# Attention in a two-layer trunk: the token norm moves from the values to the transposed weights, copies move from VectorE to ScalarE, and two query blocks share a bank and a mask

## The chip, the cores and the metric

The kernel runs on one core of a Trainium2 chip. The metric is the device time of one execution in microseconds (us). The names of the engines are those of the profile: PE is TensorE (PEld its weight loads), DVE is VectorE, ACT is ScalarE, POOL is GpSimd, SP is the queue that issues the transfers. A difference of under 0.2% of the time (2.8 us) counts here as no change.

## The reference

The model is a trunk of two layers over 512 tokens with 16 learned meta tokens ahead of them (528 columns), model width 1024. Layer 0 mixes tokens with retention and a convolution, layer 1 with the attention that this case is about, and each mixer is followed by a squared-ReLU MLP. The attention has 16 heads of width 64. Its core, cut to what matters:

```python
hn = rmsnorm(h, norm_mix_g[layer])            # one factor per token
qkv = hn @ w_qkv; q, k, v = split(qkv, 3)
q, k = rmsnorm(q, qn_g), rmsnorm(k, kn_g)     # per head
z = einsum('bhqd,bhkd->bhqk', q, k) * d ** -0.5
valid = (key < query) & (key >= n_pad)        # strictly earlier keys
log_keep = where(valid, log_sigmoid(-z), 0)
after = cumsum(log_keep, reverse) - log_keep  # keys between this one and the query
w = where(valid, exp(log_sigmoid(z) + after), 0)
out = (w @ v) @ w_o
```

So the weight of a key is the sigmoid of its score times the product of (1 - sigmoid) over the keys that lie between it and the query. The token factor of the first rmsnorm drops out of q and k, which are normed again, and stays in v.

## The kernel before, in words

The sequence is stored in reverse, channels on partitions, so that the product over the keys between becomes a running product from left to right. The 16 meta keys are the last 16 columns. There are NQ = 4 query blocks q of P = 128 queries. Block q sees the n = 528 - 128q columns from its own diagonal on: 528, 400, 272 and 144.

Products of f32 precision are made of three float32r matmuls: each operand is split into a rounded high part (`whi`, `x2h`) and the rest (`wlo`, `x2l`). In the attention DVE rounds the weights (L286) and POOL makes the low part (L289). `gemm_parts` runs one output block of 128 channels as 8 steps of k. After each step it calls `between.step`, which advances every open chain of attention work by one piece. All engines are under a manual schedule here: each works in the order in which the program records its instructions.

The attention takes the heads in pairs p = 0 to 7. `queries(p)`, `keys(p)` and `values(p)` are three gemms that start the chains; `attend(p)` runs about one pair later, between the steps of the next pair's gemms, so that PE alternates between gemm steps and pieces of attention. Which piece falls on which step is set by the table `ATT`, built from `ZS`, `TS`, `VS`, `ES` and `MS`. For head a of the pair:

- **Z(a, q)** computes the scores of one query block in a PSUM bank (`pz`): two matmuls (high and low part of Q), and one bf16 matmul of the identity `idb` with the causal mask `caus`. A block narrower than 256 columns is widened to 256. ACT turns the bank into keep (`kp`, L1266) and sigmoid (`sp`, L1267). DVE scans `kp` into the running product `E` (L1270), multiplies (`sp`, L1272), and writes the 16 meta columns twice into `Wm` (L1275).
- **T, turn(a, kb)** transposes the weights of one key block into a bank `pw` (L1283). ACT writes the high part `wTh` (L1284), DVE the low part `wTl` (L1286), which also frees the bank.
- **V** multiplies values and weights into `po` (L1293).
- **M** transposes the meta weights of both heads into `pmt` (L1299). ACT and DVE split them into `mT` (L1300, L1304). **E** adds the meta keys' part (L1307) and writes `oT`.

The pool `pat` has four banks (tag "at"), used in turn by `pq`, `pk`, `pz`, `pw`, `pv`, `pm`, `pmt` and `pe`: a fifth use waits until all readers of the first are done. The pool `pqk` has three banks for the gemms.

`token_norm` (once, in p = 0) computes the token factor `n2rb` for all 528 columns on all partitions; `values` multiplies it into `vT` as DVE reads the gemm's bank (L1204). `done(k)` runs after each k step of the last pair's values gemm: it rounds the finished head outputs `oT` of the pairs 0 to 5 into `oSh` on DVE (L1338), and POOL makes the low part `oSl` (L1339), for the output projection that follows.

## Time and profile before

| | |
|---|---|
| median of 3 runs | 1379.52 us (1379.13 to 1380.4) |
| the profiled execution's own time | 1379.57 us |
| its span | 1377.8 us |
| attention with its output projection, about | 739 to 1034 us of the span |
| one pair of heads in the steady stretch (start of mT at 794.72, 823.76, 852.80, 881.84, 910.86, 939.91) | 29.04 us |
| granted TensorE clock, mean | 0.998 |

The terms of a prediction are made against the profiled execution; 1.8 us of its time lie around the span, and it stands 0.05 us above the median. Matmuls are pipelined, so the time from the start of one to the start of the next tells what it costs, not its duration.

### The profile page before, as it was taken

The numbers are of one execution on the slowest core, as the hardware profiler recorded it, in microseconds if no ns is written. First come the engines' busy times: TensorE is split into PE (matmuls) and PEld (weight loads), VectorE is DVE, ScalarE is ACT, GpSimd is POOL, SyncE is SP. The second block draws the span as 40 slices with busy tenths as digits, with TensorE's granted clock in tenths as the row PEclk, the third lists the DMA queues.
The fourth block names the chain that finished last, engine by engine and source line by source line (L and its number), as shares of the span: only waits on it lengthen the run. The fifth ranks groups of instructions, "written<-read, shape, count | busy, mean of one in ns | idle before, by whom it ended". The sixth has DMA issues, their size and how long they took to land.

```text
span 1377.8 us, 24561 instructions
## 1 busy us (share of the span) xinstructions
PE 1356.1 (98%) x9693; PEld 1267.4 (92%) x9693; DVE 1067.4 (77%) x1909; ACT 677.8 (49%) x1328; POOL 354.6 (26%) x414
## 2 busy tenths in 40 slices
...
DMA packets 39650, 134.08 MB, mean 97 GB/s; under 512 B 4976, under 2 KB 5104, under 8 KB 39536
## 3 DMA queue, kind: packets, MB, share of 16 engines
...
q14 instruction: 38, 0.31, 0.1%
...
## 4 chain that ended last, share of the span: by engine, by line
PE 87%; DVE 8%; ACT 2%; issue 1%; DMA 0%; POOL 0%; SPq 0%; ACTq 0%; DVEq 0%; POOLq 0%
PE mm L377 50%; PE qk L377 11%; PE pz L1261 2%; PE po L1293 1%; DVE wlo L289 1%; PE pw L1283 1%; ACT whi L286 1%; PE po L796 1%; DVE x3l L415 1%; DVE mT L1304 1%; PE po L800 1%; DVE E L1270 1%; PE po L798 1%; PE pp030S L1005 0%; PE pp020S L1005 0%
## 5 line engine op out<-in xcount | busy, mean ns | idle before, releaser
L289 POOL TENSOR_TENSOR wlo<-raw,whi 128x256 fp32r<-128x256 f32 (+1 forms) x334 | 277.1, 849 | 286.6 <-ACT whi L286 133.1
L286 ACT CAST whi<-raw 128x256 fp32r<-128x256 f32 (+1 forms) x290 | 161.3, 593 | 206.1 <-PE mm L377 124.4
L592 DVE SCALAR_TENSOR_TENSOR acc<-cx,ptm,acc 128x526 f32<-128x526 f32 (+28 forms) x232 | 157.7, 742 | 3.5 <-ACT cx L587 3.5
L377 PE MATMUL mm<-xnh,whi 128*128 128x264 f32 x640 | 135.1, 293 | 0.0
L377 PE MATMUL mm<-xnl,whi 128*128 128x264 f32 x640 | 130.2, 284 | 0.4 <-DVE xnl L706 0.3
L377 PE MATMUL mm<-xnh,wlo 128*128 128x264 f32 x640 | 129.2, 283 | 0.5 <-DVE wlo L289 0.5
L289 DVE TENSOR_TENSOR wlo<-raw,whi 128x1024 fp32r<-128x1024 f32 (+1 forms) x86 | 106.5, 1239 | 18.9 <-ACT whi L286 18.0
L377 PEld LDWEIGHTS mm<-xnh,whi 128*128 128x128 f32 x640 | 100.1, 189 | 3.3 <-issue 1.3
L377 PEld LDWEIGHTS mm<-xnl,whi 128*128 128x128 f32 x640 | 99.3, 189 | 1.6 <-DVE xnl L706 1.0
L377 PEld LDWEIGHTS mm<-xnh,wlo 128*128 128x128 f32 x640 | 98.7, 188 | 0.9 <-DVE wlo L289 0.7
L241 DVE TENSOR_TENSOR wlo<-S,whi 128x512 fp32r<-128x512 f32 x96 | 65.1, 688 | 31.2 <-ACT whi L240 29.6
L240 ACT CAST whi<-S 128x512 fp32r<-128x512 f32 x96 | 57.9, 615 | 55.4 <-DVE S L225 25.5
L429 POOL TENSOR_TENSOR n2s<-n2q,n2q 128x528 f32<-128x528 f32 x1 | 1.8, 1818 | 321.5 <-DVE wlo L289 321.5
L377 PE MATMUL qk<-x2h,whi 128*128 128x264 f32 (+1 forms) x320 | 82.8, 323 | 0.5 <-ACT kraw L1153 0.5
L1030 DVE TENSOR_TENSOR h<-mm,h 128x528 f32<-128x528 f32 (+1 forms) x48 | 33.5, 699 | 62.6 <-PE mm L377 62.5
L377 PE MATMUL qk<-x2h,wlo 128*128 128x264 f32 (+1 forms) x320 | 77.0, 306 | 0.0
L377 PE MATMUL qk<-x2l,whi 128*128 128x264 f32 (+1 forms) x320 | 76.9, 305 | 0.0
L240 ACT CAST whi<-pr 128x512 fp32r<-128x512 f32 x72 | 43.3, 618 | 46.6 <-issue 10.5
L1270 DVE TENSOR_TENSOR_SCAN E<-kp,oz 128x527 f32<-128x527 f32 (+1 forms) x64 | 61.4, 979 | 1.9 <-ACT kp L1266 1.9
L377 PEld LDWEIGHTS qk<-x2h,whi 128*128 128x128 f32 x320 | 53.4, 191 | 2.6 <-ACT kraw L1153 0.9
L377 PEld LDWEIGHTS qk<-x2h,wlo 128*128 128x128 f32 x320 | 51.5, 188 | 2.7
L377 PEld LDWEIGHTS qk<-x2l,whi 128*128 128x128 f32 x320 | 51.8, 188 | 1.1
...
## 6 DMA issues: line engine op xcount, KB each, us to landing
...
```

The costliest lines, as they stand in the source:

```text
L240: nc.scalar.copy(hi[:, ks], src)
L241: nc.vector.tensor_tensor(lo[:, ks], src, hi[:, ks].bitcast(F32), ALU.subtract)
L286: copy(hi[:, ks], raw[:, ks])
L289: eng.tensor_tensor(lo[:, ks], raw[:, ks], hi[:, ks].bitcast(F32), ALU.subtract)
L377: nc.tensor.matmul(p, a[:, k, :], b[:, sl], start=(first and t == 0), stop=(last and t == 2))
L415: nc.vector.scalar_tensor_tensor(dst[1][:, :n], src, g, dst[0][:, :n].bitcast(F32), ALU.mult, ALU.subtract)
L592: nc.vector.scalar_tensor_tensor(a, cxf[:, s:T], tap(j, s), a, ALU.mult, ALU.add)
L796: nc.tensor.matmul(po[:n, :256], st[:n, :n], vk[:n], start=True, stop=Pst is None)
L798: nc.tensor.matmul(po[:n, :256], qr[:, cs], Pst, start=False, stop=True)
L1030: nc.vector.tensor_tensor(v2(h[m][:, :n], n), ps, v2(h[m][:, :n], n), ALU.add)
L1261: nc.tensor.matmul(pz[:, :w], Q2[a][:, t, q * P:(q + 1) * P], K2[a][:, k0:k0 + w], start=(t == 0), stop=(t == 1 and i > 0))
L1270: nc.vector.tensor_tensor_scan(E[:, 1:n], kp[:, :n - 1], zero.to_broadcast([P, n - 1]), 1.0, ALU.mult, ALU.add)
```

## The change

- `token_norm` no longer computes the factor for 528 columns. It computes it for five columns `rbt` with tokens on partitions: four token blocks, and one column in which the 16 meta tokens stand four times (the copy `mac` and one more matmul feed it).
- The factor is applied to the transposed weights: `wTh`, `wTl` and `mT` are scaled by a column of `rbt` as they leave PSUM. ACT's copies become activations with a scale, DVE's subtractions become scalar_tensor_tensor. `vT` becomes a plain copy, on ACT.
- The low part of `mT` is one DVE instruction over 64 partitions in place of two over 32: the columns of `Wm` are arranged so that the low parts of both heads are neighbours. The meta values `vm` are written over all 128 partitions with a 0/1 column (`CC_HM`) as scale in place of 64x64 corners.
- The `E` and `sp` tiles of the blocks 0 and 1 become one tile, and those of 2 and 3 another, so that one DVE instruction writes the meta columns of two blocks into `Wm`.
- Blocks 3 and 2 become one piece Z(a, (3, 2)): both score matrices lie side by side in one bank (144 + 272 columns, the first no longer widened to 256) under one mask matmul of 2x128 columns. The piece runs at step 2 of the table; before, block 2 ran at step 1 and block 3 at step 3.
- `done` rounds `oSh` on ACT in place of DVE.

Three places in the order of instructions, before and after. The first is in the last pair (p = 7), where `done` runs. ACT before, from the copy of the last pair's `po` on; `qy`, `qt`, `ky` and `k7t` are the keys' and queries' norms:

```order
L1310 COPY otmp_12196<-po_12151 64x512
L452 ACT_TABLE_LOAD
L452 ACTIVATE qy_12217<-qxv_11995 128x8
L453 ACTIVATE qt_12218<-qy_12217 128x8
L452 ACTIVATE ky_12221<-kxv_11997 128x528
L453 ACTIVATE k7t<-ky_12221 128x528
L1284 CAST wTh_9188<-pw_12264 128x512
L1284 CAST wTh_9187<-pw_12270 128x384
L1284 CAST wTh_9186<-pw_12275 128x256
L1266 ACT_TABLE_LOAD
```

ACT with the change:

```order
L1379 CAST oSh_12098<-oT_9194 128x512
L1343 COPY otmp_12113<-po_12068 64x512
L1379 CAST oSh_12115<-oT_9195 128x512
L454 ACT_TABLE_LOAD
L454 ACTIVATE qy_12134<-qxv_11919 128x8
L455 ACTIVATE qt_12135<-qy_12134 128x8
L454 ACTIVATE ky_12138<-kxv_11921 128x528
L455 ACTIVATE k7t<-ky_12138 128x528
L1379 CAST oSh_12144<-oT_9196 128x512
L1379 CAST oSh_12154<-oT_9197 128x512
L1379 CAST oSh_12171<-oT_9198 128x512
L1316 ACTIVATE wTh_9186<-pw_12181,rbt 128x512
```

Five of the six `oSh` copies now stand on ACT ahead of the first `wTh`; the sixth follows the third `wTh`. DVE at the same place, before:

```order
L1338 CAST oSh_12227<-oT_9198 128x512
L1338 CAST oSh_12237<-oT_9199 128x512
L456 SCALAR_TENSOR_TENSOR qt_12218<-qt_12218,qxv_11995 128x8
L457 SCALAR_TENSOR_TENSOR qy_12217<-qt_12218,qy_12217 128x8
L1177 TENSOR_SCALAR qs_12249<-qy_12217 128x8
L1178 TENSOR_SCALAR qs_12249<-qy_12217 128x8
L286 CAST whi_12165<-raw_12167 128x256
L1338 CAST oSh_12254<-oT_9200 128x512
L1180 SCALAR_TENSOR_TENSOR k7t<-k7t,kxv_11997 128x528
L1338 CAST oSh_12280<-oT_9201 128x512
L1286 TENSOR_TENSOR wTl_9192<-pw_12264,wTh_9188 128x512
```

DVE with the change:

```order
L458 SCALAR_TENSOR_TENSOR qt_12135<-qt_12135,qxv_11919 128x8
L459 SCALAR_TENSOR_TENSOR qy_12134<-qt_12135,qy_12134 128x8
L1186 TENSOR_SCALAR qs_12166<-qy_12134 128x8
L1187 TENSOR_SCALAR qs_12166<-qy_12134 128x8
L288 CAST whi_12084<-raw_12086 128x256
L1189 SCALAR_TENSOR_TENSOR k7t<-k7t,kxv_11921 128x528
L1318 SCALAR_TENSOR_TENSOR wTl_9190<-pw_12181,rbt,wTh_9186 128x512
```

The six copies are gone from ahead of `wTl` (the first two stood further up), and `wTl` reads a column of `rbt`. The second place is a pair in the steady stretch on DVE, from the keys' last scaling on, before:

```order
L1184 SCALAR_TENSOR_TENSOR ky_10956<-kraw_10739,pt,ky_10956 128x528
L1204 TENSOR_TENSOR vT<-qk_0_10912,n2rb 128x264
L1204 TENSOR_TENSOR vT<-qk_1_10913,n2rb 128x264
L1270 SCALAR_TENSOR_TENSOR E_9178<-kp_11021,oz 128x527
L1188 TENSOR_TENSOR khl_11035<-ky_10956,khl_11035 128x528
L286 CAST whi_11042<-raw_11044 128x256
L1286 TENSOR_TENSOR wTl_9189<-pw_11050,wTh_9185 128x128
L1270 SCALAR_TENSOR_TENSOR E_9179<-kp_11053,oz 128x399
L1270 SCALAR_TENSOR_TENSOR E_9180<-kp_11061,oz 128x271
L1272 TENSOR_TENSOR sp_11022<-sp_11022,E_9178 128x512
L1275 TENSOR_TENSOR Wm_9183<-sp_11022,E_9178 128x2x16
L1272 TENSOR_TENSOR sp_11054<-sp_11054,E_9179 128x384
```

With the change:

```order
L1193 SCALAR_TENSOR_TENSOR ky_10912<-kraw_10702,pt,ky_10912 128x528
L1297 SCALAR_TENSOR_TENSOR E_9178<-kp_10978,oz 128x527
L1197 TENSOR_TENSOR khl_10991<-ky_10912,khl_10991 128x528
L288 CAST whi_10998<-raw_11000 128x256
L1318 SCALAR_TENSOR_TENSOR wTl_9187<-pw_11006,rbt,wTh_9183 128x128
L1297 SCALAR_TENSOR_TENSOR E_9178<-kp_11009,oz 128x399
L1301 TENSOR_TENSOR sp_10977<-sp_10977,E_9178 128x512
L1297 SCALAR_TENSOR_TENSOR E_9179<-kp_11030,oz 128x143
L1297 SCALAR_TENSOR_TENSOR E_9179<-kp_11031,oz 128x271
L1301 TENSOR_TENSOR sp_10977<-sp_10977,E_9178 128x384
L1307 TENSOR_TENSOR Wm_9181<-sp_10977,E_9178 128x4x16
```

The two `vT` rows are gone, one `Wm` row of 4x16 stands for two of 2x16, and the scans of 143 and 271 columns come together, behind the product of block 0. The third place is PE at the scores of block 3 in a steady pair, before (block 2, with 272 columns and a mask of its own, stood two steps earlier):

```order
L377 MATMUL qk_0_10745<-x2h_8647,wlo_10490 128x264
L377 MATMUL qk_1_10746<-x2h_8647,wlo_10490 128x264
L1261 MATMUL pz_10876<-K_30_10652,Q_30_10404 128x256 x2
L1264 LDWEIGHTS idb
L1264 MATMUL pz_10876<-caus,idb 128x128
L377 MATMUL qk_0_10745<-x2h_8649,whi_10489 128x264
L377 MATMUL qk_1_10746<-x2h_8649,whi_10489 128x264
```

With the change:

```order
L379 MATMUL qk_0_10708<-x2h_8645,wlo_10461 128x264
L379 MATMUL qk_1_10709<-x2h_8645,wlo_10461 128x264
L1265 MATMUL pz_10820<-K_30_10612,Q_30_10379 128x144 x2
L1265 MATMUL pz_10820<-K_30_10612,Q_30_10379 128x272 x2
L1280 LDWEIGHTS idb
L1280 MATMUL pz_10820<-caus,idb 128x2x128
L379 MATMUL qk_0_10708<-x2h_8647,whi_10460 128x264
L379 MATMUL qk_1_10709<-x2h_8647,whi_10460 128x264
```

Block 2 has joined block 3, and one mask matmul of 2x128 columns closes both.

The diff. Left out are the lines that Z loses (they are printed above), the memsets of `mac` (in) and `vm` (out), and the column `CC_HM` of the constants, which is 1 where partition i has (i div 32) mod 2 = a, else 0:

```diff
...
-ZS, TS, VS = (0, 1, 1, 3), (10, 10, 10, 13), (16, 18)
+ZQ, ZS, TS, VS = ((0,), (1,), (3, 2)), (0, 1, 2), (10, 10, 10, 13), (16, 18)
 ATT = {}
 for a_ in range(2):
     for q_ in range(4):
-        ATT.setdefault(12 * a_ + ZS[q_], []).append(("Z", a_, q_))
+        if q_ < len(ZS):
+            ATT.setdefault(12 * a_ + ZS[q_], []).append(("Z", a_, ZQ[q_]))
         ATT.setdefault(12 * a_ + TS[q_], []).append(("T", a_, 3 - q_))
     for i_, kb_ in enumerate(((3, 2), (1, 0))):
         ATT.setdefault(12 * a_ + VS[i_], []).append(("V", a_, kb_))
...
-    Eb = [ap1.tile([P, T - P * q], F32, name=f"E{q}") for q in range(NQ)]
+    NB = [T - P * q for q in range(NQ)]
+    E2 = [ap1.tile([P, NB[q] + NB[q + 1]], F32, name=f"E{q}") for q in (0, 2)]
+    side = lambda t, q: t[:, :NB[q]] if q % 2 == 0 else t[:, NB[q - 1]:]
+    tails = lambda t, q: t[:, P:].rearrange("p (q c) -> p q c", q=2)[:, :, NB[q] - NMETA:]
+    Eb = [side(E2[q // 2], q) for q in range(NQ)]
...
     e2t = ap1.tile([P, NQ, 2], F32, name="e2t")
+    rbt = ap1.tile([P, NQ + 1], F32, name="rbt")
+    mac = ap1.tile([P, P], F32, name="mac")
...
     def values(p):
         for sl, ps in gemm_parts("w_qkv", setE, T, each=done if p == 7 else None):
-            nc.vector.tensor_tensor(vT[:, sl], ps, rb[:, sl], ALU.mult)
+            nc.scalar.copy(vT[:, sl], ps)
...
             pm = bank(f"pm{p}")
             nc.tensor.transpose(pm[:, 0:P], vT[:, SEQ:], ident)
             m = vm[p % 2]
+            mine = lambda a: ca[:, CC_HM + a:CC_HM + a + 1]
             for a in range(2):
-                r = slice(64 * a, 64 * a + 64)
-                src = pm[r, a * 64:(a + 1) * 64]
-                nc.scalar.copy(m[r, a, 0, :], src)
+                nc.scalar.activation(m[:, a, 0, :], pm[:, a * 64:(a + 1) * 64], AF.Copy, scale=mine(a))
             yield
             for a in range(2):
-                r = slice(64 * a, 64 * a + 64)
-                src = pm[r, a * 64:(a + 1) * 64]
-                nc.vector.tensor_tensor(m[r, a, 1, :], src, m[r, a, 0, :].bitcast(F32), ALU.subtract)
+                nc.vector.scalar_tensor_tensor(
+                    m[:, a, 1, :], pm[:, a * 64:(a + 1) * 64], mine(a), m[:, a, 0, :].bitcast(F32), ALU.mult, ALU.subtract)
...
-        def Z(a, q):
-
...
+        def Z(a, qs):
+            q0 = qs[0] - qs[0] % 2
+            if qs[0] != 1:
+                Ws[a, "side", q0] = ap2.tile([P, NB[q0] + NB[q0 + 1]], F32, tag=f"sp{q0}", name=f"sp{p}{a}{q0}")
+            weights_ = Ws[a, "side", q0]
+            out = []
+            for q in qs:
+                kp = ap2.tile([P, NB[q]], F32, tag=f"kp{q}", name=f"kp{p}{a}{q}", bufs=1)
+                out.append((q, NB[q], kp, side(weights_, q)))
+            def scores(pz, q, k0, w):
+                for t in range(2):
+                    nc.tensor.matmul(pz, Q2[a][:, t, q * P:(q + 1) * P], K2[a][:, k0:k0 + w],
+                                     start=(t == 0 and q == qs[0]), stop=(t == 1 and k0 >= HT and qs == (0,)))
+            def sigmoids(pz, q, kp, sg):
+                nc.scalar.activation(kp, pz, AF.Sigmoid, scale=ys[:, 0, q, a:a + 1])
+                nc.scalar.activation(sg, pz, AF.Sigmoid, scale=ys[:, 1, q, a:a + 1])
+            if len(qs) == 2:
+                pz, off = bank(f"pz{p}{a}{qs[0]}"), 0
+                for q, n, kp, sg in out:
+                    scores(pz[:, off:off + n], q, T - n, n)
+                    off += n
+                n0 = out[0][1]
+                both = pz[:, :2 * n0].rearrange("p (b c) -> p b c", b=2)[:, :, :P]
+                nc.tensor.matmul(both, idb, caus.unsqueeze(1).to_broadcast([P, 2, P]), start=False, stop=True)
+                off = 0
+                for q, n, kp, sg in out:
+                    sigmoids(pz[:, off:off + n], q, kp, sg)
+                    off += n
             else:
...
+                (q, n, kp, sg), = out
+                for i, (k0, w) in enumerate([(0, HT), (HT, HT)] if q == 0 else [(T - n, n)]):
+                    pz = bank(f"pz{p}{a}{q}{i}")[:, :w]
+                    scores(pz, q, k0, w)
+                    if i == 0:
+                        nc.tensor.matmul(pz[:, :P], idb, caus, start=False, stop=True)
+                    off = k0 if q == 0 else 0
+                    sigmoids(pz, q, kp[:, off:off + w], sg[:, off:off + w])
+            yield
+            for q, n, kp, sg in out:
+                E = Eb[q]
+                nc.vector.tensor_tensor_scan(E[:, 1:n], kp[:, :n - 1], zero.to_broadcast([P, n - 1]), 1.0, ALU.mult, ALU.add)
+            yield
+            for q, n, kp, sg in out:
+                nx, E = n - NMETA, Eb[q]
+                nc.vector.tensor_tensor(sg[:, :nx], sg[:, :nx], E[:, :nx], ALU.mult)
+                Ws[a, q] = sg
+            if qs[0]:
+                q = q0 + 1
+                twice = wm[:, q0:q0 + 2, :, a * MW:a * MW + NMETA]
+                ends = [tails(t, q).unsqueeze(2).to_broadcast([P, 2, 2, NMETA]) for t in (weights_, E2[q // 2])]
+                nc.vector.tensor_tensor(twice, *ends, ALU.mult)
         def turn(a, kb):
...
             px = bank(f"pw{p}{a}{kb}")
             for q in range(kb + 1):
                 nc.tensor.transpose(px[:, q * P:(q + 1) * P], Ws[a, q][:, (kb - q) * P:(kb - q + 1) * P], ident)
-            nc.scalar.copy(wTh[kb][:, :nq], px[:, :nq])
-            yield
-            nc.vector.tensor_tensor(wTl[kb][:, :nq], px[:, :nq], wTh[kb][:, :nq].bitcast(F32), ALU.subtract)
+            norm = rbt[:, kb:kb + 1]
+            nc.scalar.activation(wTh[kb][:, :nq], px[:, :nq], AF.Copy, scale=norm)
+            yield
+            nc.vector.scalar_tensor_tensor(
+                wTl[kb][:, :nq], px[:, :nq], norm, wTh[kb][:, :nq].bitcast(F32), ALU.mult, ALU.subtract)
         def V(a, kbs):
             if a not in po:
...
             pm = bank(f"pmt{p}")
             for q in range(NQ):
                 nc.tensor.transpose(pm[:, q * P:(q + 1) * P], wm[:, q], ident)
-            nc.scalar.copy(mT, pm)
-            yield
-            for a in range(2):
-                lo = slice(64 * a + MW, 64 * a + 2 * MW)
-                nc.vector.tensor_tensor(mT[lo], pm[lo], mT[lo].bitcast(F32), ALU.subtract)
+            norm = rbt[:, NQ:NQ + 1]
+            nc.scalar.activation(mT, pm, AF.Copy, scale=norm)
+            yield
+            lo = slice(2 * MW, 4 * MW)
+            nc.vector.scalar_tensor_tensor(mT[lo], pm[lo], norm[lo], mT[lo].bitcast(F32), ALU.mult, ALU.subtract)
         def meta(a):
             nc.tensor.matmul(po[a], vm[p % 2][:, a], mT, start=False, stop=True)
...
     def token_norm():
-        nonlocal rb, e2
-        rb, e2 = rstd(s, "n2", True, banks=(pat, "at"))
+        nonlocal e2
+        e2 = sp.tile([P, XV], F32, tag="xv", name="n2xv", bufs=1)[:, :T]
+        s.total(e2, EPS / D, EPS * EPS, (pat, "at"))
         pe = bank("pe2")
+        nc.vector.tensor_copy(mac.rearrange("p (g m) -> p g m", g=4)[:, :, :NMETA],
+                              s.acc[:, SEQ:T].unsqueeze(1).to_broadcast([P, 4, NMETA]))
         for q in range(NQ):
             nc.tensor.matmul(pe[:, q:q + 1], s.acc[:, q * P:(q + 1) * P], ones[:, 0:1], start=True, stop=True)
+        nc.tensor.matmul(pe[:, NQ:NQ + 1], mac, ones[:, 0:1], start=True, stop=True)
         for a in range(2):
             nc.vector.tensor_scalar(e2t[:, :, a], pe[:, :NQ], EPS / D, EPS * EPS, ALU.mult, ALU.add)
+        xt = ap1.tile([P, NQ + 1], F32, name="n2xt")
+        nc.vector.tensor_scalar(xt, pe[:, :NQ + 1], 1.0 / D, EPS, ALU.mult, ALU.add)
+        rsqrt(rbt, xt, [P, NQ + 1], "n2", tag="rbt")
...
         setO.append((act.tile([P, T], F32R, tag=f"Bh{k}", name=f"oSh{k}"), act.tile([P, T], F32R, tag=f"Bl{k}", name=f"oSl{k}")))
         if k < KA:
             hi, lo = (t[:, :SEQ] for t in setO[k])
-            nc.vector.tensor_copy(hi, oT[k])
+            nc.scalar.copy(hi, oT[k])
             nc.gpsimd.tensor_tensor(lo, oT[k], hi.bitcast(F32), ALU.subtract)
-    rb = e2 = None
+    e2 = None

```

More of the change, by code (lines that the diff above doesn't have):

```diff
@@ L80 @@
 CC_CAUS = CC_BLK + P
-CC_COS = CC_CAUS + P
+CC_HM = CC_CAUS + P
+CC_COS = CC_HM + 2
 CC_SIN = CC_COS + T
@@ L1087, in clear @@
         nc.gpsimd.memset(vT[:, T:], 0.0)
-        for t in (wTh[0][:, P:], wTl[0][:, P:], vm[0], vm[1]):
+        nc.gpsimd.memset(mac, 0.0)
+        for t in (wTh[0][:, P:], wTl[0][:, P:]):
             nc.gpsimd.memset(t.bitcast(F32), 0.0)
```

33 lines of the change are left out of this document (4 added, 29 removed).

## The prediction

> **What bounds the kernel now.** I read the page's first part, then the busy times of one pair's stretch, then who waited for whom on PE, and last the time order of the engines around the longest wait. The page's first part:
>
> ```profile
> PE 1356.1 (98%) x9693; PEld 1267.4 (92%) x9693; DVE 1067.4 (77%) x1909; ACT 677.8 (49%) x1328; POOL 354.6 (26%) x414
> ```
>
> Over the span PE bounds, and DVE at 77% looks unimportant. In the attention it is not. One pair of heads, busy us of PE, PEld, DVE, ACT, POOL out of 29:
>
> ```profile
> 853.50:882.50 29.00, 28.71 (x205) 25.96 (x204) 28.59 (x67) 22.18 (x51) 10.99 (x13) 1.00 0.42 111
> ```
>
> PE and DVE are both full, ACT is at 76%. Two full engines in step show waits where one hands to the other. First PE's own idle time between 740 and 1040 us, then the waits of its weight loads between 770 and 960 (total, times, longest):
>
> ```profile
> PE pz L1261 <- DVE wTl L1286: 6.2, 1, 6.2
> PE pq L1129 <- DVE mT L1304: 1.4, 6, 0.2
> ```
> ```profile
> PEld pk L1166 <- DVE ksl L1159: 2.7, 7, 1.3
> PEld pq L1129 <- ACT wTh L1284: 2.7, 6, 0.5
> PEld pmt L1299 <- DVE Wm L1275: 1.6, 6, 0.3
> ```
>
> There is one long wait of 6.2 us, and three small ones in each pair. Without the first pair's 1.3 at `pk` these are (2.7 - 1.3 + 2.7 + 1.6) / 6 = 0.95 us per pair. I put all three down to DVE: before `pq` the page names `mT` for PE itself, and `mT` holds the bank that `pq` needs.
>
> **The long wait.** PE, then DVE, then ACT in time order (start, duration, instruction, idle before):
>
> ```profile
> 957.83 0.23 PE L1264 MATMUL pz<-caus,idb 128*128 128x128 bf16 x1
> 964.31 0.81 PE L1261 MATMUL pz<-K,Q 128*128 128x264 f32 x2 [6.25 <-DVE wTl L1286]
> ```
> ```profile
> 956.64 1.29 DVE L1338 CAST oSh<-oT 128x512 fp32r<-128x512 f32 x2
> 957.86 1.22 DVE L456 SCALAR_TENSOR_TENSOR qt<-qt,qxv 128x8 f32<-128x8 f32 x1
> ...
> 962.18 1.48 DVE L1338 CAST oSh<-oT 128x512 fp32r<-128x512 f32 x1
> 963.58 0.68 DVE L1286 TENSOR_TENSOR wTl<-pw,wTh 128x512 fp32r<-128x512 f32 x1
> ```
> ```profile
> 952.24 1.28 ACT L452 ACT_TABLE_LOAD   x1
> ...
> 955.73 0.64 ACT L452 ACTIVATE ky<-kxv 128x528 f32<-128x528 f32 x1 [1.75 <-DVE kxv L1167]
> 956.41 0.65 ACT L453 ACTIVATE k7t<-ky 128x528 f32<-128x528 f32 x1
> 956.96 1.22 ACT L1284 CAST wTh<-pw 128x512 fp32r<-128x512 f32 x3
> ```
>
> The second half of block 0's scores is the fourth bank after the 512-column `pw`, so it waits until `wTl` has read that bank. `wTh` was there by 957.6; DVE came six us later, because the `oSh` copies of `done` stand in its queue. What stretches `qt`, 8 columns in 1.22 us, I read as POOL's `oSl` at work on the same memory; POOL keeps that work.
>
> With the change the copies stand on ACT, and ACT becomes what `wTl` waits for. One `oSh` falls into idle time ahead of the table load, the second moves that load by 0.6 to 952.85. It ends at 954.1, `qy` and `qt` at 954.6. `kxv` on DVE is no longer behind two copies, so `ky` and `k7t` follow until about 955.9. Three copies at 0.59 lead to 957.7, a scaled `wTh` to 958.4, `wTl` to 959.1. PE stood still from 958.06: 1.0 us would be left of 6.25. Some stretched DVE instructions remain, so I take 1.5: **a gain of 4.7**. Bounds: 0, if DVE is as late without the copies; 6.25, if nothing is left. Next behind it stand a `pw` and block 1's scores; their banks come free with `wTl` of 384 and 256 columns, within 1.0 us of the first, and PE has a gemm step of 0.7 and the scores in between, so I cost nothing there.
>
> The wait also cost clock. Windows (length, PE busy, PEld, DVE, ACT, POOL, then the granted clock):
>
> ```profile
> 960.00:962.00 2.00, 0.00 (x0) 0.00 (x0) 1.97 (x6) 0.35 (x1) 1.42 (x3) 1.00 0.00 0
> 966.00:968.00 2.00, 2.00 (x9) 1.34 (x7) 2.00 (x4) 1.34 (x6) 1.15 (x1) 0.50 0.03 8
> 968.00:970.00 2.00, 2.00 (x8) 1.64 (x8) 2.00 (x5) 1.67 (x4) 0.67 (x1) 0.71 0.78 235
> ```
>
> From 964.31 to about 968.84 (0.71 over the last window) PE worked at half clock: 4.5 / 2 = 2.3 us. At 962, four us after its last matmul, PE still had the full clock, so a wait of 1.5 us loses none: **a gain of 2.3**, or 0 if the wait stays. The Trainium skill ("TensorE: Matmul & The Clock Gate", Part 1) states that the gate halves the clock after an idle window of about 3.4 us and returns it after a busy one; the trace agrees, and by that rule any rest under 3.4 us gives the same sum.
>
> **The pairs.** Instructions of one pair on DVE, and three on ACT (count | total, mean ns | idle):
>
> ```profile
> L1275 DVE TENSOR_TENSOR Wm<-sp,E 128x32 f32<-128x32 f32 x8 | 1.4, 180 | 0.0
> L1304 DVE TENSOR_TENSOR mT<-pmt,mT 32x512 fp32r<-32x512 f32 x2 | 1.4, 690 | 0.0
> L1286 DVE TENSOR_TENSOR wTl<-pw,wTh 128x512 fp32r<-128x512 f32 x2 | 1.4, 688 | 0.0
> L1204 DVE TENSOR_TENSOR vT<-qk,n2rb 128x264 f32<-128x264 f32 x2 | 0.8, 423 | 0.0
> L1126 DVE SCALAR_TENSOR_TENSOR qhl<-qraw,pt,qhl 128x512 fp32r<-128x512 f32 x1 | 0.7, 743 | 0.0
> ```
> ```profile
> L1124 ACT ACTIVATE qhl<-qraw,pt 128x512 fp32r<-128x512 f32 x2 | 1.4, 723 | 0.1
> L1284 ACT CAST wTh<-pw 128x512 fp32r<-128x512 f32 x2 | 1.2, 586 | 0.1
> L1153 ACT COPY kraw<-qk 128x264 f32<-128x264 f32 x2 | 0.7, 382 | 0.0
> ```
>
> DVE instructions overlap by some 0.08 us, so each costs its mean less 0.08. Off DVE: two `vT`, 2 x 0.34 = 0.68; one of two `mT`, 0.69 with no overlap at its end; four of eight `Wm`, 4 x 0.10, less 0.03 on each that stays, 0.28. Onto DVE: a subtraction with a scale column. The nearest row is `qhl`, 743 against 688, so 0.055 on each of eight `wTl`, one `mT` and two `vm`: 0.6. Bounds of this: 0, and the stretched case below. DVE sheds 1.65 - 0.6 = 1.05 and would need 28.0 us per pair. The moved scans and `ksl` change places within the same sum.
>
> PE needs the measured 29.04 less its waits of 0.95, less the masks. At block 3, time order:
>
> ```profile
> 903.18 0.40 PE L1261 MATMUL pz<-K,Q 128*128 128x256 f32 x2
> 903.42 0.23 PE L1264 MATMUL pz<-caus,idb 128*128 128x128 bf16 x1
> 903.46 0.48 PE L377 MATMUL qk<-x2h,whi 128*128 128x512 f32 x1
> 903.77 0.39 PE L377 MATMUL qk<-x2l,whi 128*128 128x512 f32 x1
> 904.00 0.39 PE L377 MATMUL qk<-x2h,wlo 128*128 128x512 f32 x1
> ```
>
> A mask costs 0.04 to the next start and delays the step behind it by 0.08 (0.31 in place of 0.23). One of four per head goes, another becomes 128 columns longer (0.06 by 512 columns in 0.23): 0.06 saved per head, up to 0.14 if the longer one hides the delay; I take 0.08, 0.16 per pair. The block-3 scores go from 256 to 144 columns. The trace has no float32r matmul that narrow. From below, transposes of 128 columns, nine in 1.14 with the last one's 0.27, start every 0.11 us; from above, an f32 product of 128 columns in the retention takes two records:
>
> ```profile
> 839.02 1.14 PE L1283 MATMUL pw<-ca,sp 128*128 128x128 f32 x9
> 135.86 0.38 PE L780 MATMUL pv<-q0r,k0r 128*128 128x128 f32 x2
> ```
>
> The second of the two starts 0.11 after the first (0.38 less its own 0.27), so the product costs 0.22 at 128 columns, 0.25 at 144. Against 0.12 now (903.18 to 903.42, two matmuls) that is 0.01 less to 0.13 more each. I take no change, since all that is known of float32r here runs at the rate of single records. The Trainium skill (the same page, Part 2, LDWEIGHTS) has a load of 128 columns take 128 / 1.2 = 107 ns whatever follows. By it the narrower matmul waits for its weights, and the narrowing is worth 0.013 x 32 = 0.4 us, a sum of 1367.4; no run here shows it.
>
> The shared bank is the fourth after that of block 0's first half, which ACT has read two steps before, so it brings no new wait.
>
> So PE needs 29.04 - 0.95 - 0.16 = 27.9 and DVE 28.0. Both could gain 1.0; engines so close still wait for each other at times, and I take 0.85 in each of six pairs: **a gain of 5.1** (bounds 0.16 x 6 = 1.0 and 1.05 x 7 = 7.4).
>
> On ACT a pair gains two `vT` copies (0.38 each by `kraw`, the same shape from the same banks) and 0.14 (723 less 586) on eleven scaled copies: 2.3, which makes 24.5 of 28. I cost this at nothing, since ACT keeps 3.5 us of waiting for PE; were that cover gone, it would be up to 2.3 per pair. `vT` on ACT stands behind `khl`, as its meta copies do now; behind it wait `wTh` and the next `kp`.
>
> **The norm.** Once, at 745 us:
>
> ```profile
> 746.23 0.95 PE L1327 MATMUL pe<-ca,n2s 128*128 128x1 f32 x8
> 755.34 0.71 DVE L1159 TENSOR_TENSOR ksl<-ksq,ksh 128x528 fp32r<-128x528 f32 x1 [2.29 <-ACT ksq L1158]
> ```
>
> One more product of one column is two of eight records in 0.8 us, 0.2, and waits some 0.1 for the copy `mac`, with the keys' gemm behind it: **a loss of 0.3**. DVE's three long instructions that go here gain nothing, since DVE idles 2.29 us before its next late product anyway.
>
> **Sum.** 1379.57 - 4.7 - 2.3 - 5.1 + 0.3 = 1367.8 for the profiled execution; the median stands 0.05 below it.
>
> **Rivals.**
> (a) The narrow scores run as two-record products: 32 x 0.13 = 4.2 more, 1372.0. For it: the f32 rows do so at 128 columns. Against: one record per matmul in every float32r row.
> (b) ACT takes over DVE's lateness: the copies ahead of `wTh` hold `wTl` as long as DVE did, so wait and half clock stay, 7.0 back, 1374.8. For it: five copies ahead of it in one queue. Against: the 1.75 us that ACT idled there.
> (c) Slower: POOL stretches the scaled subtractions, which read two operands beside PSUM, as it stretched `qt`. The price is 1.22 - 0.16 at most; at half of it, 0.5, eleven per pair cost 5.5 against 1.65 shed, +3.9 x 6 = 23, less the 7.0: 1396. It decides from 0.15 each (1.65 / 11). Against it, 232 such instructions in the convolution, PSUM and a column in, with POOL busy:
>
> ```profile
> L592 DVE SCALAR_TENSOR_TENSOR acc<-cx,ptm,acc 128x526 f32<-128x526 f32 (+28 forms) x232 | 157.7, 742 | 3.5 <-ACT cx L587 3.5
> ```
>
> (d) The change gives PE nothing in the pairs because ACT's extra 2.3 us arrive late on the same hand-overs, and (b) besides: of all gains the masks' 1.0 is left, 1379.57 + 0.3 - 1.0 = 1378.9, no change. For it: ACT would be at 88%. Against: at `pq` the page names `mT` on DVE for PE itself.
>
> **How the numbers follow.** The forecast gets 0.72, (a) 0.09, (b) 0.09, (c) 0.05, (d) 0.05. The first three cases are faster by over 0.2% (2.8 us, about what a measurement can tell from no change): 0.90; same 0.05; slower 0.05. The lower end takes 1.05 in seven pairs, the whole 6.25, the 2.3 and the first pair's 1.3: 1379.6 - 17.2 + 0.3 = 1362.7, so 1362. The upper end holds (a) and (b): 1375.
>
> **What would show it.** In the changed profile the row of PE's `pz` waiting for `wTl` should be under 2.5 us with the clock at 1.00 throughout 957 to 980; `pq` waiting for `mT` should be gone; the distance of two `mT` should be 28.0 to 28.4 us; DVE's busy share of a pair should be about 97%. Two 144-column scores should start 0.10 to 0.13 apart; 0.25 would be (a). A long wait of PE for `wTl` with ACT's `wTh` just ahead of it would be (b), a mean of `wTl` over 0.85 us at 512 columns (c). The prediction is wrong if the pairs still take 29 us.

## The result

The changed kernel takes 1370.74 us (median, 1370.28 to 1371.12) against 1379.96 for the kernel before in the same comparison: a ratio of 0.9932, interval 0.9918 to 0.9946, or 9.2 us less. Forecast were 1367.8, 11.8 less. The profiled execution took 1370.59, its span is 1368.8.

The page's first part after the change, and one pair's stretch (length, PE, PEld, DVE, ACT, POOL busy, granted clock, DMA):

```profile
PE 1351.1 (99%) x9679; PEld 1261.0 (92%) x9679; DVE 1052.7 (77%) x1848; ACT 691.4 (51%) x1350; POOL 364.4 (27%) x413
```
```profile
853.50:882.50 29.00, 29.00 (x211) 26.84 (x210) 28.14 (x64) 24.51 (x54) 11.92 (x12) 1.00 0.41 123
```

The waits of PE's own between 740 and 1040 us. The long wait for `wTl` is halved, `pq`'s wait for `mT` is gone, and `pmt` has a new one:

```profile
PE pz L1265 <- DVE wTl L1318: 3.2, 1, 3.2
PE pmt L1332 <- DVE Wm L1307: 1.4, 2, 1.1
```

Of the three small waits that PE's weight loads had in each pair (770 to 960 us) only the first pair's `pk` is left:

```profile
PEld pk L1175 <- DVE ksl L1168: 1.1, 1, 1.1
```

Where the time came from is read off one instruction that each pair has once: ACT's `mT`, here for the pairs 0, 5, 6 and 7, before and after:

```profile
793.61 0.59 ACT L1300 CAST mT<-pmt 128x512 fp32r<-128x512 f32 x1 [1.56 <-PE pmt L1299]
938.80 0.59 ACT L1300 CAST mT<-pmt 128x512 fp32r<-128x512 f32 x1 [1.63 <-PE pmt L1299]
976.24 0.59 ACT L1300 CAST mT<-pmt 128x512 fp32r<-128x512 f32 x1 [1.39 <-PE pmt L1299]
1002.24 0.59 ACT L1300 CAST mT<-pmt 128x512 fp32r<-128x512 f32 x1 [4.59 <-PE pmt L1299]
```
```profile
793.90 0.69 ACT L1334 ACTIVATE mT<-pmt,rbt 128x512 fp32r<-128x512 f32 x1 [1.31 <-PE pmt L1332]
933.75 0.69 ACT L1334 ACTIVATE mT<-pmt,rbt 128x512 fp32r<-128x512 f32 x1 [1.32 <-PE pmt L1332]
966.93 0.69 ACT L1334 ACTIVATE mT<-pmt,rbt 128x512 fp32r<-128x512 f32 x1 [2.61 <-PE pmt L1332]
992.91 0.69 ACT L1334 ACTIVATE mT<-pmt,rbt 128x512 fp32r<-128x512 f32 x1 [4.52 <-PE pmt L1332]
```

Up to pair 0 the changed kernel is 0.3 us late. A pair is (938.80 - 793.61) / 5 = 29.04 before and (933.75 - 793.90) / 5 = 27.97 after, 1.07 less. From pair 5 to pair 6 it is 37.44 before, 8.40 more than a pair, and 33.18 after, 5.21 more. This is the stretch of pair 7's values gemm with `done` and the first output blocks (the expectations below call it the last pair's). From pair 6 to pair 7 it is 26.00 and 25.98. So the gain is 6 x 1.07 = 6.4 in the pairs and 8.40 - 5.21 = 3.2 in that stretch, less 0.3 ahead of them: 9.3 up to pair 7. The spans differ by 9.0, since what follows is 0.3 longer (375.56 before, 375.89 after); why was not looked into.

The same distances for every kernel of this study, read in the same way (us). The times come from five comparisons, in which the kernel before took 1379.76 to 1380.03:

| kernel | time, median | a pair | 5 to 6 | 6 to 7 |
|---|---|---|---|---|
| before | 1379.96 | 29.04 | 37.44 | 26.00 |
| changed | 1370.74 | 27.97 | 33.18 | 25.98 |
| b_osh | 1377.58 | 29.03 | 34.24 | 26.93 |
| u_osh | 1374.43 | 27.93 | 37.02 | 25.84 |
| no_osl | 1367.63 | 27.94 | 29.85 | 26.02 |
| tiny_pool | 1371.47 | 27.94 | 33.50 | 25.92 |
| late_small | 1375.25 | 28.44 | 33.05 | 27.36 |
| u_vt | 1371.21 | 27.98 | 33.10 | 25.98 |
| no_mt | 1371.53 | 28.02 | 33.21 | 25.85 |
| u_vt_mt | 1376.31 | 28.72 | 33.89 | 26.80 |
| u_bank | 1371.55 | 28.01 | 33.15 | 26.13 |
| u_clear | 1370.15 | 27.95 | 33.13 | 26.14 |
| best | 1370.76 | 27.97 | 31.94 | 27.44 |
| best2 | 1369.36 | 27.96 | 31.89 | 26.04 |

**The long wait after the change.** PE, then DVE, POOL and ACT in time order:

```profile
952.06 0.23 PE L1291 MATMUL pz<-caus,idb 128*128 128x128 bf16 x1
955.47 0.51 PE L1265 MATMUL pz<-K,Q 128*128 128x264 f32 x2 [3.18 <-DVE wTl L1318]
...
965.67 0.41 PE L1332 MATMUL pmt<-ca,Wm 128*128 128x128 f32 x2 [1.07 <-DVE Wm L1307]
```
```profile
949.50 1.27 DVE L458 SCALAR_TENSOR_TENSOR qt<-qt,qxv 128x8 f32<-128x8 f32 x1
950.80 0.66 DVE L459 SCALAR_TENSOR_TENSOR qy<-qt,qy 128x8 f32<-128x8 f32 x1
951.49 1.21 DVE L1186 TENSOR_SCALAR qs<-qy 128x8 f32<-128x8 f32 x1
952.62 1.32 DVE L1187 TENSOR_SCALAR qs<-qy 128x8 f32<-128x8 f32 x1
...
954.67 1.66 DVE L1318 SCALAR_TENSOR_TENSOR wTl<-pw,rbt,wTh 128x512 fp32r<-128x512 f32 x3
```
```profile
948.13 2.61 POOL L1380 TENSOR_TENSOR oSl<-oT,oSh 128x512 fp32r<-128x512 f32 x2
...
951.40 2.51 POOL L1380 TENSOR_TENSOR oSl<-oT,oSh 128x512 fp32r<-128x512 f32 x2
```
```profile
950.16 1.65 ACT L1379 CAST oSh<-oT 128x512 fp32r<-128x512 f32 x3
951.71 1.51 ACT L1316 ACTIVATE wTh<-pw,rbt 128x512 fp32r<-128x512 f32 x3
```

ACT brought the first `wTh` (0.69 in the pairs) at 952.4, 0.1 after PE's last matmul was done; the prediction had 0.3. DVE came to `wTl` only at 954.67. The copies are gone from its queue, but four instructions of eight columns hold it 4.5 us. They end when POOL's instructions end: `qt` at 950.77 and the second `oSl` of its row at 950.74, the last `qs` at 953.94 and that of the next row at 953.91.

**The start.** The last sum `n2s` on POOL, before and after, and PE's wait for it:

```profile
743.84 1.34 POOL L429 TENSOR_TENSOR n2s<-n2s,n2q 128x528 f32<-128x528 f32 x1
```
```profile
744.32 1.33 POOL L431 TENSOR_TENSOR n2s<-n2s,n2q 128x528 f32<-128x528 f32 x1
```
```profile
745.71 1.16 PE L444 MATMUL n2ps<-n2s,ca 128*128 128x264 f32 x4 [0.45 <-POOL n2s L431]
```

The change had moved a fourth `wlo` ahead of this sum on POOL, which the prediction did not look at.

### The profile page after: what moved, and what is told of

Read it like the earlier page. It is cut to its first block, busy times and chain, and to the rows that moved or that the text cites. A ratio compares the mean times of both kernels' runs of the same rounds, so it can differ in the third digit from the quotient of the medians.

```text
span 1368.8 us, 24471 instructions
## 1 busy us (share of the span) xinstructions
PE 1351.1 (99%) x9679; PEld 1261.0 (92%) x9679; DVE 1052.7 (77%) x1848; ACT 691.4 (51%) x1350; POOL 364.4 (27%) x413
## 3 DMA queue, kind: packets, MB, share of 16 engines
q8 instruction: 76, 1.25, 0.4%
## 5 line engine op out<-in xcount | busy, mean ns | idle before, releaser
L291 POOL TENSOR_TENSOR wlo<-raw,whi 128x256 fp32r<-128x256 f32 (+1 forms) x334 | 287.6, 881 | 268.2 <-ACT whi L288 133.6
```

What stands on the lines that cost most here:

```text
L291: eng.tensor_tensor(lo[:, ks], raw[:, ks], hi[:, ks].bitcast(F32), ALU.subtract)
```

## The experiments

### The copies and the long wait

u_osh undoes one part of the change, b_osh does this part alone:

```diff
-            nc.scalar.copy(hi, oT[k])         # u_osh, in the changed kernel
+            nc.vector.tensor_copy(hi, oT[k])
-            nc.vector.tensor_copy(hi, oT[k])  # b_osh, in the kernel before
+            nc.scalar.copy(hi, oT[k])
```

> The changed kernel with one part undone: the copies oSh of done stand on DVE again. If the copies' place is what shortened the long wait (theory), PE's wait of pz for wTl goes from 3.2 back to about 6 us, the granted clock falls to a half behind it, and the time is 1370.7 + 3 + 2.3 = 1376 us (1374 to 1377.5). If the wait was shortened by something else in the change, such as less other work on DVE (rival), the wait stays under 4 us at full clock and the time is under 1372.

> The kernel before with one part of the change alone: the copies oSh on ACT. Theory: the long wait falls from 6.25 to 3 to 3.5 and the half clock behind it goes: 1379.9 - 3 - 2.3 = 1374.6 us (1373.5 to 1376), the pairs still 29.0 us apart. Rival: the wait needs the rest of the change too (less DVE work ahead of it), stays over 5 us with the half clock, and the time is 1378 or more.

Measured: u_osh 1374.43 (ratio 0.9962, 0.9948 to 0.9977), b_osh 1377.58 (0.9984, 0.9975 to 0.9994). The wait in u_osh, the wait in b_osh, and a window of b_osh behind it (the clock stands third from the end):

```profile
958.57 0.81 PE L1265 MATMUL pz<-K,Q 128*128 128x264 f32 x2 [6.71 <-DVE wTl L1318]
```
```profile
961.43 0.81 PE L1261 MATMUL pz<-K,Q 128*128 128x264 f32 x2 [2.93 <-DVE wTl L1286]
```
```profile
961.00:963.00 2.00, 1.57 (x5) 1.38 (x6) 2.00 (x4) 1.37 (x4) 2.00 (x3) 0.52 0.00 0
```

The theory holds in its cause: the place of the copies makes the long wait. It fails in its sizes. In the changed kernel the copies are worth 3.7 us and not 5.3 (1374.43 lies low in the range expected), since u_osh has no wait at `pmt`: what PE waits less at `pz`, it waits in part there. Alone they are worth 2.2 and not 5.3: the wait fell by 3.3 as expected, but the half clock came all the same, after a wait of 2.9 us, and 0.9 went in the following distance, where PE waits 0.7 at `po` for `mT`. The stretch from pair 5 to pair 6 is 5.21 over a pair in b_osh (34.24 - 29.03) as in the changed kernel: what the change gains in this stretch, the copies gain alone.

no_osl leaves `oSl` out, tiny_pool takes the four small instructions from DVE in the last pair:

```diff
-            nc.gpsimd.tensor_tensor(lo, oT[k], hi.bitcast(F32), ALU.subtract)   # no_osl
+            setO[k] = (setO[k][0], setO[k][0])
-            rsqrt_newton(qy, qt, qxv)            # tiny_pool, for p == 7:
+            small = nc.gpsimd                    # Newton as 2 tensor_scalar, 2 tensor_tensor,
+            small.tensor_scalar(qt, qt, -0.5, None, ALU.mult)
...
+            small.tensor_scalar(ys[:, 0], qy, -0.125, None, ALU.mult)
```

> The changed kernel without the subtractions oSl that done gives to POOL; the products that read oSl read oSh a second time, so PE's work is the same and the low halves of those six pairs are not in the output. If POOL's subtractions hold DVE's small instructions (theory), qt, qy and the two qs fall from 0.66 to 1.32 us each to about 0.2, the wait of pz for wTl falls from 3.2 to 0.5 to 1.0, the 1.4 us of pmt waiting for Wm behind it to under 0.5, and the time is 1366 to 1368.5. If what is left of the wait is ACT's copies ahead of wTh (rival), the wait stays over 2.5 and the time is 1370 or more.

> The changed kernel with the last pair's four small instructions (the Newton step of qy and the two qs) as six on POOL in place of DVE; POOL keeps oSl. Theory (DVE's lateness at the long wait is those four, 4.5 us held by POOL): the wait of pz for wTl falls from 3.2 to 0.5 to 1.5, pmt's wait for Wm to under 0.7, and the time is 1367 to 1369. Rival: the next DVE instructions (whi, k7t) are held in their place, the wait falls by 1 us at most, and the time is 1369.8 or more.

Measured: no_osl 1367.63 (0.9914, 0.9900 to 0.9929), tiny_pool 1371.47 (0.9943, 0.9928 to 0.9957). Two small instructions and the wait in no_osl; then, in tiny_pool, PE's longest total wait and POOL's `qy`:

```profile
948.92 0.38 DVE L458 SCALAR_TENSOR_TENSOR qt<-qt,qxv 128x8 f32<-128x8 f32 x1 [0.46 <-ACT qt L455]
...
949.53 0.17 DVE L1186 TENSOR_SCALAR qs<-qy 128x8 f32<-128x8 f32 x1
```
```profile
953.07 0.51 PE L1265 MATMUL pz<-K,Q 128*128 128x264 f32 x2 [0.91 <-DVE wTl L1318]
```
```profile
PE qk L379 <- POOL oSl L1388: 2.2, 2, 1.9
```
```profile
958.59 1.21 POOL L1190 TENSOR_TENSOR qy<-qt,qy 128x8 f32<-128x8 f32 x1
```

Without `oSl` all of the theory comes true: `qs` takes 0.17, the wait is 0.91, `pmt` waits no more, the stretch is 3.3 us shorter. So ACT's copies ahead of `wTh` leave 0.9 of the wait, close to the 1.0 of the prediction's working, and POOL's holding of DVE made the rest; PE itself waited for no `oSl` in the changed kernel. With the small instructions on POOL the wait fell too (0.95), but the rival was right about the time: now POOL is held (`qy` ends at 959.80 with DVE's scan `E`), `oSl` comes late, and PE waits 2.2 us for it in the output projection's first block. DVE is held again as well, only later: beside this `oSl` a product `sp` takes 1.69, two scans 2.66 and the next `sp` 1.02, in place of 0.66, 1.06 and 0.53.

late_small moves them in every pair behind `khl`:

```diff
             yield from wait(KW[1])
-            rsqrt_newton(qy, qt, qxv)
-            ys = ...                     # and the two qs
...
             nc.vector.tensor_tensor(hl[:, 1], y, hl[:, 0].bitcast(F32), ALU.subtract)
+            rsqrt_newton(qy, qt, qxv)
+            ys = ...                     # and the two qs
```

> The changed kernel with qy's Newton step and the two qs of every pair moved behind khl in the keys' chain, so that in the last pair DVE reaches them after POOL's oSl and wTl ahead of them; nothing is left out and no engine gets other work. Theory (the small instructions, held by POOL, are what keeps DVE from wTl): they take 0.2 us each where they now stand, the wait of pz for wTl falls from 3.2 to 0.5 to 1.5, and the time is 1367 to 1369. Rival: as when those four went to POOL, what is won at pz is given back later, at pmt or in the last gemm, and the time is 1370 or more. The pairs stay 28.0 us apart under both.

Measured: 1375.25 (0.9968, 0.9956 to 0.9980), and both theories wrong on the pairs, which went to 28.44. Waits of PE's weight loads between 790 and 940 us, and the place on DVE that the small instructions had left:

```profile
PEld pmt L1332 <- DVE Wm L1307: 3.4, 6, 0.6
```
```profile
896.16 0.89 DVE L1185 SCALAR_TENSOR_TENSOR k5t<-k5t,kxv 128x528 f32<-128x528 f32 x1 [0.99 <-ACT k5t L455]
```

In their old place they fill a time in which DVE waits for ACT anyway; in the new one they stand ahead of `Wm`, and PE waits 0.6 per pair for it. No engine got other work, and a pair costs 0.47 more. At `pz` the wait fell to 0.95, as in tiny_pool, and again most of it came back: the stretch is 4.6 over a pair (33.05 - 28.44) against 5.2, with a wait of 1.8 at `pmt`. Behind that the clock fell to a half (0.50 from 971 to 973), and the last distance is 27.36.

### What bounds a pair

u_vt puts the copies `vT` back on DVE, no_mt leaves out the subtraction `mT`, u_vt_mt undoes both reliefs; u_bank undoes the shared bank and mask:

```diff
-            nc.scalar.copy(vT[:, sl], ps)            # u_vt, u_vt_mt
+            nc.vector.tensor_copy(vT[:, sl], ps)
-            lo = slice(2 * MW, 4 * MW)               # u_vt_mt: in two; no_mt: neither
+            for a in range(2):
+                lo = slice(2 * MW + a * MW, 3 * MW + a * MW)
-ZQ, ZS, TS, VS = ((0,), (1,), (3, 2)), (0, 1, 2), ...          # u_bank
+ZQ, ZS, TS, VS = ((0,), (1,), (3,), (2,)), (0, 1, 2, 2), ...
```

> The changed kernel with the copies vT back on DVE (a plain copy). DVE is busy 97% of a 27.98 us pair, which is 27.1; with 0.68 more it is 27.8. Theory (PE bounds the pairs now, but DVE stands just under it): the pairs go to 28.1 to 28.5 us, waits of PE for mT or ksl come back, and the time is 1371.5 to 1375. Rival (DVE has room): the pairs stay at 28.0 and the time is under 1371.3.

> The changed kernel without the subtraction mT on DVE, 0.68 to 0.76 us less per pair; the meta keys' low rows then hold the high rows' values, so their low halves are not in the output. Theory (PE bounds the pairs): the pairs stay at 27.9 to 28.0 us, and only the last pair gains, 0 to 1 us: 1369.5 to 1371. Rival (DVE still sets the pair): the pairs go to 27.3 to 27.7 and the time is 1368.5 or less.

> The changed kernel with two of DVE's reliefs undone at once: the copies vT on DVE, and the subtraction mT as two of 32 rows. DVE's work in a pair of 27.98 us goes from 27.1 to 27.1 + 0.68 + 0.68 = 28.5. Theory (below PE's 27.98 DVE's work costs nothing, above it each us costs one): the pairs go to 28.3 to 28.8, waits of PE for DVE come back, and the time is 1373 to 1377. Rival (what shortened the pairs is the new order of the scores and of the meta weights, not DVE's work): the pairs stay under 28.1 and the time under 1372.

> The changed kernel with the shared bank undone: blocks 3 and 2 have a bank and a 128-column mask each, the scores stay 144 and 272 columns wide. Theory (the prediction's price of the mask, 0.08 per head on a PE that bounds the pair): the pairs go from 27.98 to 28.14 us (28.04 to 28.26), the time up by 1.1, to 1371.8 (1371.2 to 1372.8). Rival: the mask is hidden behind other waits, the pairs stay within 0.03 of 27.98 and the time within 0.5.

Measured: u_vt 1371.21 (0.9938, 0.9923 to 0.9953), no_mt 1371.53 (0.9941, 0.9924 to 0.9957), u_vt_mt 1376.31 (0.9972, 0.9961 to 0.9982), u_bank 1371.55 (0.9940, 0.9926 to 0.9955). The same window as above in u_vt and u_vt_mt, and a wait of PE in u_vt_mt:

```profile
853.50:882.50 29.00, 29.00 (x211) 26.80 (x209) 28.51 (x66) 23.94 (x52) 12.76 (x12) 1.00 0.42 123
```
```profile
853.50:882.50 29.00, 28.59 (x207) 26.09 (x205) 28.50 (x64) 23.34 (x51) 13.04 (x13) 1.00 0.41 111
```
```profile
PE pq L1138 <- DVE mT L1338: 2.5, 6, 0.4
```

no_mt shows that PE sets the pair now: with 0.7 us less on DVE the pairs stay where they were (28.02). Its time is 0.5 above the range expected, and 0.8 above the changed kernel, too little to tell. u_vt_mt shows the edge on the other side: with both reliefs undone the pairs are 28.72 and `pq` waits for `mT` again, as the theory had it. No run undoes the subtraction `mT` alone. Done in two it also holds `pq`'s bank longer (1.52 in place of 0.76), so whether the 0.75 is DVE's whole work or this one bank is not separated. And 28.72 is still 0.32 under 29.04, which is left for the rest of the change and was not taken apart. u_vt stands between, and the rival was right: DVE had room for another 0.68. Its busy time rose by only 0.37 in 29 us. Part of the 97% was waiting, and for POOL; a `wlo` on POOL and the scan `E` in the changed kernel, then the scan in u_vt:

```profile
869.44 1.19 POOL L291 TENSOR_TENSOR wlo<-raw,whi 128x256 fp32r<-128x256 f32 x1 [2.20 <-DVE whi L288]
```
```profile
870.24 1.50 DVE L1297 TENSOR_TENSOR_SCAN E<-kp,oz 128x527 f32<-128x527 f32 x1 [0.20 <-ACT kp L1269]
```
```profile
870.73 1.24 DVE L1297 TENSOR_TENSOR_SCAN E<-kp,oz 128x527 f32<-128x527 f32 x1
```

With `vT` on ACT, DVE is free early, waits 0.20 for `kp`, and its scan meets the `wlo`, which ends at 870.63. Between 800 and 942 us the five scans of 527 columns that meet one so take 1.50 or 1.51, the six that meet none 1.25 or 1.26. With `vT` on DVE the scan starts when that `wlo` is done (870.72) and takes 1.24. `kp` itself comes no later with `vT` on ACT: at 870.20, and in u_vt at 870.30. So of the change's parts the move of `vT` gave the pairs nothing as long as the rest stands.

u_bank met neither forecast in full: its time is up by 0.8, its pairs by less than the theory said. They are 0.04 above the changed kernel's and 0.08 above the least of the same pairs in other runs (27.93), about the spread: the mask is worth 0.1 us per pair at most, not clearly more than nothing. Its scores show what a narrow score costs alone, against the shared bank (below):

```profile
773.58 0.34 PE L1265 MATMUL pz<-K,Q 128*128 128x144 f32 x2
773.76 0.23 PE L1291 MATMUL pz<-caus,idb 128*128 128x128 bf16 x1
```
```profile
773.03 0.64 PE L1265 MATMUL pz<-K,Q 128*128 128x144 f32 x4
773.51 0.28 PE L1280 MATMUL pz<-caus,idb 128*128 128x256 bf16 x1
```

Two of 144 columns take 0.18, or 0.09 each; two of 144 and two of 272 take 0.48.

### POOL's order, the clock, and a faster version

u_clear keeps the memsets of `vm`; best adds two edits, best2 one more:

```diff
-        for t in (wTh[0][:, P:], wTl[0][:, P:]):                  # u_clear, best, best2
+        for t in (wTh[0][:, P:], wTl[0][:, P:], vm[0], vm[1]):
+            if p == 7:                                            # best, best2: not on DVE,
+                nc.scalar.activation(ys[:, 0], qy, AF.Copy, scale=-0.125)   # but behind k7t
+                nc.scalar.activation(ys[:, 1], qy, AF.Copy, scale=0.125)
+        if p < 1:                          # best, best2: end of attend; done takes oS for k = 0
+            nc.scalar.copy(oS[0], Ws["sum"])
+            yield
+            nc.gpsimd.tensor_tensor(oS[1], Ws["sum"], oS[0].bitcast(F32), ALU.subtract)
+ATT6.setdefault(MS + 1, []).append(("M",))           # best2: ATT6 replaces ATT for p == 6
+ATT6.setdefault(ES[0] + 1, []).append(("E", 0))
```

> The changed kernel with the two memsets of vm kept on POOL; POOL's order ahead of the attention changes with them: two wlo in place of four stand ahead of the last sum n2s, the other two behind it. Theory (part of what the norm costs is that the change put a wlo ahead of n2s): n2s starts up to 0.6 us earlier, PE's wait of n2ps for n2s, 0.45, goes, and the stretch from the end of x2's gemm to the first pair's mT is 0.3 to 0.6 shorter; the time is 1370.0 to 1370.7, within what can be told from no change. Rival: the wait stays, since PE's order or n2q sets it.

> The changed kernel with three edits against what is left: vm's memsets kept as in the run on POOL's order; the last pair's two qs on ACT, behind wTh, in place of DVE; and pair 0's output split into its two halves after pair 0 already, so that five and not six splits stand in the last values gemm. Theory: DVE loses some 2.5 us of held instructions ahead of wTl and POOL 1.3 us of oSl; the wait of pz falls from 3.2 to 1.0 to 2.0, the last pair's 33.2 us to 31 to 32.3, and the time is 1368 to 1369.8. Rival: the hold only passes on to the next instructions (whi, k7t, E), as it did for two runs before; the last pair stays over 32.7 and the time is 1370 or more.

> The last run (best) with the meta weights' transpose pmt and the meta output po of pair 6 one gemm step later, so that PE has a step of w_oa to do while DVE brings Wm. In best PE waited 1.8 us at pmt and then ran 3.4 us at half clock (1.7 lost) with nothing left to wait for behind it. Theory (in this stretch PE's waits and its clock are one account: what DVE is late by): with one step of 0.7 us moved into the wait, 0.5 to 1.1 of the wait stays, the clock stays full, and the time is 1368.3 to 1369.6. Rival (the clock falls in some window of this stretch whatever is moved, or po then waits for mT as long): 1370.2 or more.

Measured: u_clear 1370.15 (1369.88 to 1370.21; ratio 0.9927, 0.9914 to 0.9941), best 1370.76 (0.9931, 0.9918 to 0.9943), best2 1369.36 (0.9924, 0.9910 to 0.9937).

u_clear: POOL's sum starts at 742.85, PE no longer waits for it, and pair 0's `mT` starts at 793.19, 0.7 ahead of the changed kernel. The time follows by 0.6, too little for the intervals to tell. Its trace shows one thing more. The long wait is as long as in the changed kernel, but here the clock fell behind it:

```profile
742.85 1.80 POOL L431 TENSOR_TENSOR n2s<-n2s,n2q 128x528 f32<-128x528 f32 x1
```
```profile
954.62 0.81 PE L1265 MATMUL pz<-K,Q 128*128 128x264 f32 x2 [3.15 <-DVE wTl L1318]
```
```profile
954.00:956.00 2.00, 1.38 (x4) 1.28 (x5) 2.00 (x4) 1.60 (x5) 2.00 (x3) 0.66 0.00 0
956.00:958.00 2.00, 2.00 (x7) 1.35 (x6) 2.00 (x3) 0.32 (x1) 1.77 (x2) 0.50 0.00 0
```

PE lost some 1.7 us to the half clock, and the stretch is 33.13 against 33.18: nothing. In its place the 1.4 us of waiting at `pmt` are gone. DVE is busy all of these windows (2.00 of 2.00), and PE comes to `Wm` late or waits for it.

best: the wait fell from 3.2 to 0.9 and the stretch to 31.94, as the theory had it. The time did not fall, because this time the clock fell behind the stretch. PE's wait, and three windows around and behind it:

```profile
964.02 0.41 PE L1337 MATMUL pmt<-ca,Wm 128*128 128x128 f32 x2 [1.39 <-DVE Wm L1312]
```
```profile
964.00:966.00 2.00, 1.61 (x8) 1.20 (x9) 2.00 (x7) 0.69 (x1) 1.84 (x2) 0.88 0.02 8
966.00:968.00 2.00, 2.00 (x8) 1.60 (x7) 1.97 (x6) 0.00 (x0) 1.49 (x3) 0.50 0.00 0
968.00:970.00 2.00, 2.00 (x12) 1.82 (x11) 1.36 (x4) 1.58 (x3) 0.94 (x2) 0.77 0.81 252
```

Two waits of 1.39 and 0.37 were enough, and behind them PE waits for nobody, so the lost time counts: 27.44 in place of 26.0. best2 gives PE one gemm step to do in that wait. PE waits 1.1 at `pmt`, the clock stays full, the distance is 26.04, and the time is 1.4 under best and under the changed kernel, as expected:

```profile
PE pmt L1341 <- DVE Wm L1316: 1.1, 2, 0.7
```
```profile
964.00:966.00 2.00, 1.63 (x10) 1.21 (x11) 2.00 (x7) 0.69 (x1) 1.90 (x2) 1.00 0.00 1
```

best2 is the fastest kernel of this study that leaves nothing out. Its interval overlaps that of the changed kernel, and 1.4 us count as no change by the measure of the start; only the traces carry the difference.

## Why the prediction was right, and where not

Right in direction and within its range, 2.9 us too low. That it came so close is in part luck: the long wait and its clock were put 3.8 too high, the pairs 1.3 too low.

- **The long wait, 4.7, and the half clock, 2.3.** Together 3.2 were gained and not 7.0. ACT's part of the working was right: it leaves 0.9 to 1.0 (no_osl). The step that failed is "Some stretched DVE instructions remain, so I take 1.5". The four small ones were 3.6 us longer than without `oSl`, and 3.2 of the wait stayed. Then 1.4 came back at `pmt`, where I had costed nothing behind the wait beyond `pw` and block 1's scores: `Wm`, eleven microseconds later in DVE's queue, was not looked at. The Trainium skill ("SBUF — State Buffer", "SBUF: two separate sides") states that DVE and POOL share a port pair that one instruction holds for its whole length, the other being blocked; a DVE instruction that reads two operands from there, or runs in a two-port mode, needs the pair. By it each small instruction ends with POOL's, and the rows agree (within 0.03 us). I had read the stretching off `qt` but spread it thinly instead of counting one POOL instruction for each.
- **The clock as a gain of its own.** u_clear and the changed kernel have the same wait and the same stretch, one at half clock and one at full. So have u_vt and u_bank at half clock (waits of 3.09 and 3.13) and no_mt at full (3.15): from pair 5 to pair 6 all five take 33.10 to 33.21. The 2.3 us were PE's (2.4, since a clock of 0.71 over 968 to 970 puts the end at 969.16 and not at 968.84), but in this stretch DVE was the later one, so the two terms could not be added. "A wait of 1.5 us loses none" was not safe either: best lost it after 1.8 us in two parts.
- **The pairs, 5.1.** 6.4 were gained. PE's 27.9 was right (27.93 to 28.0); DVE's 28.0 was not. It was made from the pair's 29.04 less what was shed, as if DVE had been busy all of it, and so the two engines seemed level. DVE had at least 0.68 to spare (u_vt). With PE's own 1.11 in six pairs and none taken off for hand-overs the term would have been 6.7.
- **The masks, 0.16 per pair,** were at most 0.1 (u_bank).
- **The narrow scores** run at single records, as taken; rival (a) is out. The load of 128 columns in 107 ns that the Trainium skill states ("TensorE: Matmul & The Clock Gate", Part 2, LDWEIGHTS) does not set the spacing here: 0.09 us each in u_bank. What the narrowing gives the whole was not measured apart.
- **ACT's 2.3 us at nothing** was right: `vT` on ACT or on DVE gives the same pairs (u_vt), and `kp` comes no later for it.
- **The norm, 0.3,** came out as 0.3 at pair 0, but of other parts: the extra product cost 0.22 as taken (747.52 to 747.74) and waited for nothing, POOL's order ahead of `n2s` cost 0.48, which u_clear takes back, and 0.4 of the sum was regained before pair 0's `mT`.
- **Rivals.** (b), ACT taking over the lateness, did not come: ACT was there at 952.4 and DVE at 954.67. (c) did not come: `wTl`, which reads PSUM and one SBUF operand, took 1.66 for three beside `oSl` as in the pairs without. (d) is out with the pairs.

Of the tests stated, `pq` for `mT`, the distance of two `mT`, DVE's 97%, the scores and `wTl` (0.75) came as said or just under it (27.97 for 28.0, scores 0.09 apart for 0.10); the wait under 2.5 us did not, and it was the one that counted.
